# Contrast kernel on one core: the first 8 KB of each row as four row-interleaved loads, and tiles 6 to 11 loaded in pairs

## The chip, the core and the metric

The kernel runs on one core of a Trainium2 chip. The metric is device time in microseconds (us); before the change it is 239.09 us, the median of three runs (239.09 to 239.23). A profile shows one execution of the program, with its own span.

## What is computed

The input is 16 x 3 images of 512 x 512 float32. Each image is stretched about its own mean by a factor of 1.5 and clipped to 0..1:

```python
mean = np.mean(x, axis=(2, 3), keepdims=True)
return np.clip(mean + factor * (x - mean), 0, 1).astype(np.float32)
```

So an image's mean must be complete before its first pixel can be written. Input and output are 50.33 MB each, and every byte is moved once in each direction.

## The kernel before

**Tiles.** The 48 images are cut into 12 tiles of four images. A tile is 128 partitions (32 for each image) of one 8192-element row each, so 32 KB a partition and 4 MB (4096 KB) in all. The on-chip memory holds `ring`, six such tiles; tile t lies in slot t % 6, is loaded there, is changed in place and is stored from there.

**Work on one tile** (`compute`, lines 78 to 98). VectorE (DVE) adds up the first 4352 elements of each row (L81) while ScalarE (ACT) adds up the other 3840 (L84). Two small matmuls (L86, L87) against a constant block matrix add the sums of the 32 partitions of each image and give each partition its shift, (1 - factor) x mean. DVE then does multiply-and-add (L91) and clip (L94) over the whole row, and ACT issues the store (L101). For tile 0 alone the last three steps are done in two parts, of 2048 and 6144 elements. DVE and ACT take the tiles in order; ACT's instruction stream for a tile is sum, store, and then the sum of the next tile.

**Loads** (`load`, lines 68 to 76). All loads are issued by SyncE (SP) on one DMA queue (q1 in the profile), in the order written out by hand in lines 104 to 112; all stores are issued by ACT on a second queue (q10). Each load is one DMA with one completion: whoever reads any part of it waits until all of it has landed. With `n=2` one DMA fills two neighbouring slots, so both tiles count as landed together. At the start come five loads: the first 2048 elements of tile 0's rows, the other 6144, tile 1, tiles 2 and 3 as one, tiles 4 and 5 as one. Tile t + 6 goes to the slot of tile t, so its load must wait until the store of tile t has landed; it is written after `compute(t)`, for t = 0 to 5, which makes six single loads. SP executes in order: a load that waits holds up all later loads.

In what follows S8 is the store of tile 8, L8 the load of tile 8, and L4/5 a load of tiles 4 and 5 in one DMA. (The profile's own labels such as L81 are lines of the kernel; all of these are 63 or higher.)

Of the kernel before, what the change touches and what calls it, by code (L numbers as in the profile page):

```python
# [1 line left out]

# [4 lines left out]


P = 128  # L10
ROW = 8192
BUFS = 6
SHORT = 2048
FIRST = (SHORT, ROW - SHORT)
SUM = 4352


@with_exitstack
def kernel(
    ctx: ExitStack,  # L20
    tc: tile.TileContext,
    x: bass.AP,
    factor: float,
    out: bass.AP,
):

    nc = tc.nc
    f32 = mybir.dt.float32  # L30
    Alu = mybir.AluOpType
    Act = mybir.ActivationFunctionType

    B, C, H, W = x.shape
    n_img, n_pix = B * C, H * W
    ppi = n_pix // ROW
    per_tile = P // ppi
    n_tiles = n_img // per_tile
    assert ppi * ROW == n_pix and per_tile * n_tiles == n_img

    factor = float(factor)
    wconst = (1.0 - factor) / float(n_pix)

    x_f = x.rearrange("b c h w -> (b c h w)")
    out_f = out.rearrange("b c h w -> (b c h w)")

    def dram(ap, t, c0=0, c1=ROW):
        return bass.AP(tensor=ap.tensor, offset=t * P * ROW + c0, ap=[[ROW, P], [1, c1 - c0]])

    consts = ctx.enter_context(tc.tile_pool(name="consts", bufs=1))  # L50
    xpool = ctx.enter_context(tc.tile_pool(name="xpool", bufs=1))
    small = ctx.enter_context(tc.tile_pool(name="small", bufs=1))
    psum = ctx.enter_context(tc.tile_pool(name="psum", bufs=1, space=bass.MemoryType.PSUM))


    sums = small.tile([P, 2 * n_tiles], f32, name="sums")
    junk = small.tile([P, ROW - SUM], f32, name="junk")
    bias = psum.tile([P, n_tiles], f32, name="bias")

    blockw = consts.tile([P, P], f32, name="blockw")  # L60
    nc.gpsimd.memset(blockw, 0.0)  # L61
    for a in range(0, P, ppi):
        nc.gpsimd.memset(blockw[a : a + ppi, a : a + ppi], wconst)  # L63


    ring = xpool.tile([P, BUFS, ROW], f32, name="ring")

    def load(t, c0=0, c1=ROW, n=1):

        b = t % BUFS  # L70
        src = bass.AP(
            tensor=x_f.tensor,
            offset=t * P * ROW + c0,
            ap=[[ROW, P], [P * ROW, n], [1, c1 - c0]],
        )
        nc.sync.dma_start(out=ring[:, b : b + n, c0:c1], in_=src)  # L76

    def compute(t):
        xt = ring[:, t % BUFS, :]
        own = sums[:, 2 * t : 2 * t + 2]  # L80
        nc.vector.tensor_reduce(  # L81
            out=own[:, 0:1], in_=xt[:, 0:SUM], axis=mybir.AxisListType.X, op=Alu.add
        )
        nc.scalar.activation(out=junk, in_=xt[:, SUM:ROW], func=Act.Copy, accum_out=own[:, 1:2])  # L84
        shift = bias[:, t : t + 1]
        nc.tensor.matmul(shift, blockw, own[:, 1:2], start=True, stop=False)  # L86
        nc.tensor.matmul(shift, blockw, own[:, 0:1], start=False, stop=True)  # L87
        c = 0
        for n in FIRST if t == 0 else [ROW]:
            part = xt[:, c : c + n]  # L90
            nc.vector.tensor_scalar(  # L91
                out=part, in0=part, scalar1=factor, scalar2=shift, op0=Alu.mult, op1=Alu.add
            )
            nc.vector.tensor_scalar(  # L94
                out=part, in0=part, scalar1=0.0, scalar2=1.0, op0=Alu.max, op1=Alu.min
            )
            store(t, c, c + n)
            c += n

    def store(t, c0, c1):  # L100
        nc.scalar.dma_start(out=dram(out_f, t, c0, c1), in_=ring[:, t % BUFS, c0:c1])  # L101

    with tc.manual_schedule():
        load(0, c1=SHORT)
        load(0, c0=SHORT)
        load(1)
        load(2, n=2)
        load(4, n=2)
        for t in range(n_tiles):
            compute(t)  # L110
            if t + BUFS < n_tiles:
                load(t + BUFS)


# [1 line left out]
_INS = ['x', 'factor']  # L116
_OUTS = [((16, 3, 512, 512), 'float32')]

_NUMBERS = {'factor': 1.5}


# [26 lines left out]
```

## Time and profile before

| | us |
|---|---|
| median of 3 runs | 239.09 |
| span of the profiled execution | 237.3 |
| DVE busy in it | 163.1 (69%) |
| ACT busy | 43.2 (18%) |
| PE (matmul) busy | 14.1 (6%) |
| DMA queue q1 (loads), share of the 16 DMA engines' time | 49.7% |
| DMA queue q10 (stores) | 49.2% |
| DMA bytes, mean rate | 100.66 MB, 424 GB/s |

The profiled execution's span begins with the program's first instruction on the engines and ends with the last. The median, of other executions, lies 1.8 us above that span (239.09 - 237.27). A busy time is the sum over instructions; for DMA, the profile gives the share of the time of the 16 DMA engines, and for each issue the time from the issue to the landing of its last byte ("to landing"). The chain is followed backwards from the last instruction of the compute engines to whatever released it.

The landings, each from the DMA-issues view narrowed to one issue (issue time plus time to landing):

| DMA | issued | landed | | DMA | issued | landed |
|---|---|---|---|---|---|---|
| tile 0, first 8 KB | 0.74 | 5.5 | | S0, second part | 27.6 | 55.8 |
| L2/3 | 2.1 | 50.6 | | S1 | 41.9 | 76.4 |
| L4/5 | 2.8 | 87.6 | | S2 | 65.1 | 95.9 |
| L6 | 56.0 | 107.0 | | S3 | 79.4 | 115.2 |
| L7 | 76.6 | 126.2 | | S4 | 102.0 | 134.6 |
| L8 | 96.0 | 145.7 | | S5 | 116.3 | 154.0 |
| L9 | 115.3 | 165.0 | | S6 | 130.6 | 173.4 |
| L10 | 134.7 | 184.4 | | S7 | 144.9 | 192.8 |
| L11 | 154.2 | 203.7 | | S8 | 160.1 | 207.4 |
| | | | | S9 | 179.4 | 217.1 |
| | | | | S10 | 198.8 | 226.8 |
| | | | | S11 | 218.2 | 236.5 |

### The profile page before, as it was taken

What the parts mean: (1) busy time and instruction counts of PE and PEld (TensorE: products, weight loads), DVE (VectorE), ACT (ScalarE), POOL (GpSimd) and SP (SyncE); (2) the same over time, 40 slices, a digit from 0 to 9 for tenths busy, and PEclk for the clock granted to TensorE, in tenths of its full rate; (3) what the DMA queues carried; (4) which work ended last, traced back from release to release, by engine and by line L of the source; (5) the groups of instructions that cost most, each with busy time, mean ns of one, the idle gap of its engine ahead of it and who ended that gap; (6) DMA issues with size and microseconds to landing.
All of it is one profiled execution on the core that took longest, in us unless ns stands there. A gap on an engine that the chain in (4) does not pass through costs nothing.

```text
span 237.3 us, 285 instructions
## 1 busy us (share of the span) xinstructions
PE 14.1 (6%) x48; PEld 12.0 (5%) x48; DVE 163.1 (69%) x38; ACT 43.2 (18%) x25; POOL 0.9 (0%) x9
## 2 busy tenths in 40 slices
PE   0010010001010001010010100100100100010000
PEld 0010010001010001010010100100100100010000
DVE  0079989048989328999989898891892795687000
ACT  2050230041050023050320504101400500500000
POOL 1000000000000000000000000000000000000000
DMA  7999999999999999999999999999999999999996
GB/s 297 410 442 442 421 442 359 456 439 441 442 436 414 403 431 442 442 442 442 436 442 436 414 409 425 442 442 442 442 436 442 436 420 403 425 442 442 442 442 265
DMA packets 3712, 100.66 MB, mean 424 GB/s; under 512 B 384, under 2 KB 384, under 8 KB 384
## 3 DMA queue, kind: packets, MB, share of 16 engines
q1 hardware_dynamic: 1840, 50.33, 49.7%
q10 hardware_dynamic: 1872, 50.33, 49.2%
HBM read 50.33 MB, written 50.33 MB: 424 GB/s over the span
## 4 chain that ended last, share of the span: by engine, by line
DMA 57%; DVE 29%; another core or an unknown queue 3%; PE 1%; SPq 1%; issue 0%; DVEq 0%
DMA ring<-in_x_dram 41%; DMA out_dram<-ring 16%; DVE sums L81 10%; DVE ring L91 9%; DVE ring L94 9%; PE bias L87 1%; SPq L76 1%; DVEq L91 0%
## 5 line engine op out<-in xcount | busy, mean ns | idle before, releaser
L81 DVE TENSOR_REDUCE sums<-ring 128x1 f32<-128x4352 f32 x12 | 56.2, 4683 | 45.7 <-DMA ring<-in_x_dram 45.7
L84 ACT ACTIVATE junk<-ring 128x3840 f32<-128x3840 f32 x12 | 40.8, 3403 | 163.3 <-DMA ring<-in_x_dram 107.5
L91 DVE TENSOR_SCALAR ring<-ring,bias 128x8192 f32<-128x8192 f32 (+2 forms) x13 | 54.1, 4163 | 8.9 <-PE bias L87 7.4
L94 DVE TENSOR_SCALAR ring<-ring 128x8192 f32<-128x8192 f32 (+2 forms) x13 | 53.3, 4099 | 0.4
L86 PE MATMUL bias<-sums,blockw 128*128 128x1 f32 x24 | 7.0, 361 | 190.8 <-ACT junk L84 190.8
L86 PEld LDWEIGHTS bias<-sums,blockw 128*128 128x128 f32 x24 | 6.0, 312 | 191.7 <-ACT junk L84 175.2
L87 PE MATMUL bias<-sums,blockw 128*128 128x1 f32 x24 | 7.0, 363 | 4.3 <-DVE sums L81 3.9
L87 PEld LDWEIGHTS bias<-sums,blockw 128*128 128x128 f32 x24 | 6.0, 311 | 5.3 <-DVE sums L81 5.0
L84 ACT ACTIVATION_READ_ACCUMULATOR junk<-ring 128x1 f32 x12 | 2.2, 186 | 0.0
L84 ACT ACT_TABLE_LOAD x1 | 1.3, 1283 | 0.7 <-PEq L129 0.7
L63 POOL MEMSET blockw<- 32x32 f32 x4 | 0.5, 117 | 0.2
L61 POOL MEMSET blockw<- 128x128 f32 x1 | 0.2, 204 | 0.3 <-POOLq L129 0.3
L129 POOL MEMSET const-bfloat16-1.0<- 128x1 bf16 x1 | 0.1, 111 | 0.0
L129 POOL MEMSET const-uint8-127<- 128x1 uint8 x1 | 0.1, 111 | 0.0
L129 POOL MEMSET const-float32-1.0<- 128x1 f32 x1 | 0.1, 108 | 0.0
L129 POOL MEMSET const-float32-0.0<- 128x1 f32 x1 | 0.1, 103 | 0.2 <-issue 0.2
## 6 DMA issues: line engine op xcount, KB each, us to landing
out_dram<-ring ACTq DMA_DIRECT2D x11, 4096.0 KB, 35.8
ring<-in_x_dram SPq DMA_DIRECT2D x7, 4096.0 KB, 49.7
ring<-in_x_dram SPq DMA_DIRECT2D x2, 8192.0 KB, 66.7
ring<-in_x_dram SPq DMA_DIRECT2D x1, 3072.0 KB, 11.7
out_dram<-ring ACTq DMA_DIRECT2D x1, 3072.0 KB, 28.2
ring<-in_x_dram SPq DMA_DIRECT2D x1, 1024.0 KB, 4.8
out_dram<-ring ACTq DMA_DIRECT2D x1, 1024.0 KB, 17.5
```

The lines of the kernel that those rows point to most:

```text
L61: nc.gpsimd.memset(blockw, 0.0)
L63: nc.gpsimd.memset(blockw[a : a + ppi, a : a + ppi], wconst)
L76: nc.sync.dma_start(out=ring[:, b : b + n, c0:c1], in_=src)
L81: nc.vector.tensor_reduce(out=own[:, 0:1], in_=xt[:, 0:SUM], axis=mybir.AxisListType.X, op=Alu.add)
L84: nc.scalar.activation(out=junk, in_=xt[:, SUM:ROW], func=Act.Copy, accum_out=own[:, 1:2])
L86: nc.tensor.matmul(shift, blockw, own[:, 1:2], start=True, stop=False)
L87: nc.tensor.matmul(shift, blockw, own[:, 0:1], start=False, stop=True)
L91: nc.vector.tensor_scalar(out=part, in0=part, scalar1=factor, scalar2=shift, op0=Alu.mult, op1=Alu.add)
L94: nc.vector.tensor_scalar(out=part, in0=part, scalar1=0.0, scalar2=1.0, op0=Alu.max, op1=Alu.min)
L129: nc = _bacc.Bacc("TRN2", target_bir_lowering=False, num_devices=1)
```

## The change

Two things change, both in the loads. The first load of tile 0 (2048 elements of each of 128 rows, 1 MB) becomes four loads of 32 rows each, rows f, f+4, f+8 and so on for f = 0 to 3, 256 KB each. And the six single loads of tiles 6 to 11 become three loads of two tiles each, written after `compute(1)`, `compute(3)` and `compute(5)`. The work of the other engines is unchanged.

```diff
+STEP = 4
...
-    def load(t, c0=0, c1=ROW, n=1):
+    def load(t, c0=0, c1=ROW, n=1, first=0, step=1):
...
-            offset=t * P * ROW + c0,
-            ap=[[ROW, P], [P * ROW, n], [1, c1 - c0]],
+            offset=(t * P + first) * ROW + c0,
+            ap=[[step * ROW, P // step], [P * ROW, n], [1, c1 - c0]],
...
-        nc.sync.dma_start(out=ring[:, b : b + n, c0:c1], in_=src)
+        nc.sync.dma_start(out=ring[first:P:step, b : b + n, c0:c1], in_=src)
...
-        load(0, c1=SHORT)
+        for first in range(STEP):
+            load(0, c1=SHORT, first=first, step=STEP)
         load(0, c0=SHORT)
         load(1)
         load(2, n=2)
         load(4, n=2)
         for t in range(n_tiles):
             compute(t)
-            if t + BUFS < n_tiles:
-                load(t + BUFS)
+            if t % 2 and t + BUFS < n_tiles:
+                load(t + BUFS - 1, n=2)
```

In the compiled order of the changed kernel SP issues eleven loads, as many as before: four of 32x2048, one of 128x6144, one of 128x8192 and five of 128x2x8192. The load of tiles 4 and 5 also gains a wait for one of the four quarter loads, whose semaphore it uses again.

## The prediction

> **What bounds the kernel now.** I read the page first, for busy shares and the slices.
>
> ```profile
> span 237.3 us, 285 instructions
> ...
> DVE  0079989048989328999989898891892795687000
> ...
> DMA  7999999999999999999999999999999999999996
> GB/s 297 410 442 442 421 442 359 456 439 441 442 436 414 403 431 442 442 442 442 436 442 436 414 409 425 442 442 442 442 436 442 436 420 403 425 442 442 442 442 265
> ```
>
> The DMA engines have work in every slice, the last included, while DVE is idle in the last three. So the span is 100.66 MB pushed through full DMA engines, with a short start and a short end. Next, how fast they can go: the windows view (length, busy times, clock, DMA share, GB/s) and the DMA view of 107 to 202 us (packets, MB, share of the engines).
>
> ```profile
> 56.00:203.80 147.80, 9.39 (x33) 8.02 (x32) 117.43 (x27) 27.97 (x16) 0.00 (x0) 1.00 1.00 433
> 203.80:236.50 32.70, 1.18 (x4) 1.01 (x4) 13.56 (x3) 3.50 (x2) 0.00 (x0) 1.00 0.97 417
> ```
>
> ```profile
> q10 hardware_dynamic: 717, 20.87, 50.9%
> q1 hardware_dynamic: 703, 20.48, 49.9%
> ```
>
> While loads and stores are both queued, they share 433 GB/s half and half. The loads end at 203.7 (L11). From then on only stores are left, and they still fill 0.97 of the engines, because a backlog is waiting: S8 lands at 207.4, S9 at 217.1, S10 at 226.8, S11 at 236.5, 9.7 us apart, which is 4.19 MB at 433 GB/s. That backlog is what hides the work on the last tile. Last, the chain in order of time (start, length, what) and the timeline (start, length, engine, line; in brackets the idle time before).
>
> ```profile
> 154.17 49.57 DMA ring<-in_x_dram
> 203.73 0.02 issue
> 203.76 4.70 DVE sums L81
> ...
> 213.71 4.43 DVE ring L94
> ```
>
> ```profile
> 50.67 4.69 DVE L81 TENSOR_REDUCE sums<-ring 128x1 f32<-128x4352 f32 x1 [8.77 <-DMA ring<-in_x_dram]
> ...
> 102.00 0.34 ACTq L101 DMA_DIRECT2D out_dram<-ring  x1
> ...
> 116.30 0.34 ACTq L101 DMA_DIRECT2D out_dram<-ring  x1
> ```
>
> Tile 11 lands at 203.7 and its store is issued at 218.2: 14.4 us of work. S10, issued at 198.8, keeps the engines busy until 226.8, so S11 is in the queue 8.6 us before it is due. The start at 50.67 shows what a pair does: DVE had waited 8.77 us for L2/3, and tile 2 could not start before tile 3 had landed too. Two tiles that land together are worked on one after the other: L4/5 lands at 87.6, S4 goes out at 102.0, S5 at 116.3, so the second store is issued 28.7 us after the landing.
>
> **Part 1: pairs, the middle.** L6/7 must wait for S0 and S1, so it is issued when L7 was, at 76.6, not at 56.0. The load queue does not run dry: L4/5 occupies it until 87.6, 11 us longer. Likewise L8/9 goes out with S3's landing at 115.3, 10.9 us before L6/7 lands (126.2), and L10/11 at 154.2, 10.8 us before 165.0. Nothing is queued behind them on SP but the next such load. The loads thus keep their half share and L10/11 lands when L11 did, at 203.7. Tiles 6, 8 and 10 become available 19.4 us later than now (126.2, 165.0, 203.7 against 107.0, 145.7, 184.4).
>
> The stores follow: S6 at 126.2 + 14.4 = 140.6, S7 at 154.9, S8 at 179.4, S9 at 193.7. The store queue has work until S5 lands (154.0), S7 (192.8), S9 (217.1), so each pair's first store is 13 us early; this slack is the cover, and it costs nothing here. Three SP issues go away (0.34 us each), hidden behind a queue that is never empty: nothing.
>
> **Part 1: pairs, the end.** Here the cover is gone. Tiles 10 and 11 land together at 203.7. S10 is issued 14.4 us later, at 218.2, 1.1 us after S9 has landed: the engines stand idle. S11 is issued at 203.7 + 28.7 = 232.5, where DVE is now the bound. S10, alone, is through by about 218.2 + 2 + 9.7 = 230, so S11 also starts on idle engines and must pay in full the time from issue to landing.
>
> The trace has no store on idle engines. Its nearest row is the first load: issued at 0.74, 1 MB landed after 4.8 us, of which 2.4 us is 1.05 MB at 433 GB/s, which leaves 2.4 us. Counted by the bytes instead (254 GB/s from 2 to 3 us, 449 from 3 to 5.5, 1.38 MB by 5.5), the stream runs as if at full rate from 2.4, 1.7 us after the issue. So 1.7 to 2.4; I take **2.0**, since a store of 4 MB has room to even out its start. The tail after the last landing is 237.3 - 236.5 = 0.8.
>
> The sum: 203.7 + 28.7 + 2.0 + 9.7 + 0.8 = **244.9** as span, 7.6 over the profiled 237.3. The median lies 1.8 above that span, so 239.1 + 7.6 = **246.7**.
>
> **Part 2: the quarter loads.** The same bytes in four DMAs. SP's first issues start 0.46 us apart (0.74, 1.17, 1.64, 2.11), so three more put back the second load of tile 0 from 1.2 to 2.6. Its bytes are due when the first MB is through, at 5.5, 2.9 us after its issue, against 1.7 to 2.4 of latency: hidden, with 0.5 us to spare. If that cover is gone it costs at most 3 x 0.46 = 1.4. The other way, the first MB lands 0.7 us later than a stream at full rate would have it (2.4 against 1.7 above); a finer split can win back no more. I take nothing, between -0.7 and +1.4, since both ends are far from any row of a 32-row DMA and the stream is fed throughout. No compute waits for less than the whole of tile 0 (L81 and L84 read both parts), so no work starts earlier. L4/5's new wait ends with a quarter load, near 5 us, and its bytes are due at 50.6: nothing. The three additional semaphores that L81 waits for on tile 0 fall into the wait for the second part.
>
> [...] Back-to-back DMAs in the trace show no gap: the last four stores land 9.7 us apart, at full rate. [...]
>
> **Rivals.**
>
> *The loads win a larger share* (not slower). If pairs got more than half of the engines, L10/11 would land earlier and the stores' backlog would be longer. To hide both last tiles, S11 must be issued 2.0 us before S10 ends in an unbroken queue, at 226.8 - 2.0 = 224.8, so L10/11 must land at 196.1, 7.6 us earlier. From then on the bytes decide again: 239.1, or 238.4 with the start's 0.7. For it: L4/5 took 50.6 to 87.6 = 37.0 us, against 38.7 for two single loads. Against it: until 55.8 it ran beside tile 0's smaller store parts, and L10/11 would need 50.3 MB - 25.2 MB in 108.5 us in place of 116.1, 232 GB/s, 54% of the engines, where the view shows 49.9. Chance 4%.
>
> *Tile 10 does not wait for tile 11*, so the change does not do what it says: then S10 leaves at about 198.8, and it stays 239.1. Against it: the 8.77 us before tile 2. Chance 2%.
>
> *The quarter loads are lopsided*: 32 rows spread over only half of the engines. These would carry twice their share of the first MB, 2.4 us more, and every later landing waits for the slowest engine: 246.7 + 2.4 = 249.1. For it: no row shows a 32-row load. Against it: 32 divides by 16 as 128 does. Chance 8%. Something dearer at the start, beyond 249: 3%.
>
> **How the numbers follow.** The forecast, 246.7, has 83%. Its own bounds: store latency -0.3/+0.4, start -0.7/+1.4, and the loads' share at an even 50% in place of 49.9 of 100.8 (half a percent of 116 us, so 0.6 earlier): 245.1 to 248.5. The range is 245.1 to 249.1, which takes in the lopsided start. This kernel's measurement tells about 0.2% (0.5 us) from no change. Faster by more than that: 3%, most of the larger-share case, with the start's gain; same: 3%, the rest of that case and the one where tile 10 does not wait; slower: 94%.
>
> **What would show it.** Right: L6/7, L8/9, L10/11 issued near 76.6, 115.3 and 154.2; DVE idle about 10 us before tile 6; L10/11 landing near 203.7; store issues near 218.2 and 232.5; the DMA slices broken near 218 and 231, and the chain ending with two tiles of DVE work. Wrong: an L10/11 that lands more than 1 us off 203.7 (the share), a tile 0 that lands well after 12.9 (the start), S11 landing much over 12 us after its issue (the latency), or no gap between the last stores.

## The result and the profile after

The changed kernel takes 246.16 us (median of six runs, 244.66 to 246.92), against 239.22 us before (239.09 to 239.38): 1.0282 times the time, 95% interval 1.0255 to 1.0309. It is slower, by 6.9 us. Its profiled execution has a span of 242.7 us and is the fastest of the six; the other spans lie between 243.2 and 245.0. The page of the changed kernel, its span and slices:

```profile
span 242.7 us, 282 instructions
...
DVE  0048989238989428989408998607998806898900
...
DMA  6999999999999999999999999999999999999496
GB/s 213 385 428 432 398 432 439 448 420 444 432 432 432 432 432 432 437 432 432 432 432 432 432 432 432 432 432 432 437 432 437 432 432 437 437 421 432 178 421 270
```

The middle is as full as before (433 GB/s from 56 to 203 us in both). New are the weak first slices (213 and 385 GB/s, were 297 and 410) and the hole near the end (178 GB/s, digit 4), with VectorE (DVE) busy above it. The windows of the changed kernel (length, busy times, clock, DMA share, GB/s) show both; 449 GB/s was the rate of the first row's window before.

```profile
3.00:5.50 2.50, 0.00 (x0) 0.00 (x0) 0.00 (x0) 0.00 (x0) 0.00 (x0) 1.00 0.86 292
...
219.00:229.00 10.00, 1.17 (x4) 1.00 (x4) 9.23 (x3) 1.41 (x2) 0.00 (x0) 1.00 0.77 331
229.00:231.50 2.50, 0.00 (x0) 0.00 (x0) 1.78 (x1) 0.00 (x0) 0.00 (x0) 1.00 0.00 0
```

From 229.0 to 231.5 no packet starts: S10 landed at 228.7 and the DMA engines wait for tile 11. (A packet is counted in the window in which it starts, so the share of a short window can be over 1.00.) The timeline of the changed kernel tells why (the end of each line is the idle time before and what ended it):

```profile
127.09 4.69 DVE L82 TENSOR_REDUCE sums<-ring 128x1 f32<-128x4352 f32 x1 [8.87 <-DMA ring<-in_x_dram]
...
164.60 4.69 DVE L82 TENSOR_REDUCE sums<-ring 128x1 f32<-128x4352 f32 x1 [8.85 <-DMA ring<-in_x_dram]
...
202.11 4.69 DVE L82 TENSOR_REDUCE sums<-ring 128x1 f32<-128x4352 f32 x1 [8.85 <-DMA ring<-in_x_dram]
...
216.52 0.34 ACTq L102 DMA_DIRECT2D out_dram<-ring  x1
...
230.81 0.34 ACTq L102 DMA_DIRECT2D out_dram<-ring  x1
```

The three pairs land at 127.1, 164.6 and 202.1, DVE idle 8.9 us before each. S10 goes out 14.4 us after the last landing, S11 28.7 us after it. S10 leaves 2.6 us before S9 has landed (219.1), so the engines run through to it without a hole; the one hole is the one before S11. The DMA-issues view narrowed to S11:

```profile
out_dram<-ring ACTq DMA_DIRECT2D x1, 4096.0 KB, 11.1
```

230.8 + 11.1 = 241.9, and the span ends 0.8 later. The chain of this profile reaches back only to 221.1, to the last two DVE steps of tile 11; what stands before them has to be read from the timeline.

### The profile page after: what moved, and what is told of

Its sections match the earlier page's. It is cut to its first block, busy times and chain, and to the rows that moved or that the text cites. A ratio compares the mean times of both kernels' runs of the same rounds, so it can differ in the third digit from the quotient of the medians.

```text
span 242.7 us, 282 instructions
## 1 busy us (share of the span) xinstructions
PE 14.0 (6%) x48; PEld 12.0 (5%) x48; DVE 163.0 (67%) x38; ACT 43.2 (18%) x25; POOL 0.9 (0%) x9
```

## The experiments

Each time stands beside the kernel before, measured on the same chip in the same series (239.2 to 239.3 us). Differences below are between medians.

### The two parts alone: pairs_only and quarters_only

`pairs_only` is the changed kernel with the first load undone, `quarters_only` the one with the pairs undone:

```diff
 pairs_only
-        for first in range(STEP):
-            load(0, c1=SHORT, first=first, step=STEP)
+        load(0, c1=SHORT)
 quarters_only
-            if t % 2 and t + BUFS < n_tiles:
-                load(t + BUFS - 1, n=2)
+            if t + BUFS < n_tiles:
+                load(t + BUFS)
```

> Pairs for tiles 6 to 11, the first load whole as before. Theory A (the quarter loads lost about 2 us at the start, and the pairs cost the rest at the end): L10/11 lands near 200.0, that is 2.1 before the 202.1 of the changed kernel, S11 is issued 28.7 later, near 228.7, the span is near 240.6 and the time near 242.5 to 244. Theory B (the quarters cost nothing, the pairs everything): the span of the changed kernel again, 242.7, and its time, 246.2.

> Quarter loads of the first MB, single loads for tiles 6 to 11. Theory A: the stores' backlog still covers the last tile, the bytes decide, and the 2.0 to 2.3 us by which tile 0 came later (15.2 against 12.9) are paid in full: 241.2 to 241.5. Theory B: 239.2.

Measured: pairs_only 242.97 us (241.3 to 243.1), ratio 1.0142 (1.0117 to 1.0167); quarters_only 243.0 us (242.21 to 243.64), ratio 1.0154 (1.0135 to 1.0174). Each part alone costs 3.8 us, and theory B is out: the quarters cost as much as the pairs. In pairs_only the pair lands where theory A had it; its timeline:

```profile
125.24 4.69 DVE L82 TENSOR_REDUCE sums<-ring 128x1 f32<-128x4352 f32 x1 [8.82 <-DMA ring<-in_x_dram]
...
162.76 4.68 DVE L82 TENSOR_REDUCE sums<-ring 128x1 f32<-128x4352 f32 x1 [8.86 <-DMA ring<-in_x_dram]
...
200.34 4.69 DVE L82 TENSOR_REDUCE sums<-ring 128x1 f32<-128x4352 f32 x1 [8.92 <-DMA ring<-in_x_dram]
...
229.04 0.34 ACTq L102 DMA_DIRECT2D out_dram<-ring  x1
```

Two readings: the pairs come 37.5 us apart, where two single loads took 38.7 (2 x 19.4), so that L10/11 lands at 200.3 and not at 203.7; and S11 again goes out 28.7 us after that.

quarters_only lost more than the 2.0 to 2.3 that I had read off the landing of tile 0. Its last microseconds show where the rest is, first of quarters_only and then of before:

```profile
226.00:234.00 8.00, 0.00 (x0) 0.00 (x0) 0.00 (x0) 0.00 (x0) 0.00 (x0) 1.00 1.02 442
234.00:236.00 2.00, 0.00 (x0) 0.00 (x0) 0.00 (x0) 0.00 (x0) 0.00 (x0) 1.00 0.91 393
236.00:238.00 2.00, 0.00 (x0) 0.00 (x0) 0.00 (x0) 0.00 (x0) 0.00 (x0) 1.00 0.46 197
```

```profile
234.00:235.00 1.00, 0.00 (x0) 0.00 (x0) 0.00 (x0) 0.00 (x0) 0.00 (x0) 1.00 1.21 524
235.00:236.50 1.50, 0.00 (x0) 0.00 (x0) 0.00 (x0) 0.00 (x0) 0.00 (x0) 1.00 0.01 0
```

Before, all 16 DMA engines stop within 0.6 us of each other (the table below). With the quarters some have finished while others have several packets left, and the rate falls away over some 3 us. The last store is done when the slowest engine is done: that engine finishes S11 3.0 us later than before, the fastest one 0.4, and the span is 3.6 longer.

### How the first load is split: block_quarters, halves_only, column_quarters

`block_quarters` takes 32 neighbouring rows at a time, `halves_only` has two loads of every second row (`STEP = 2`), `column_quarters` has four loads of all 128 rows. All have single loads for tiles 6 to 11.

```diff
 block_quarters
-        for first in range(STEP):
-            load(0, c1=SHORT, first=first, step=STEP)
+        for first in range(0, P, P // STEP):
+            load(0, c1=SHORT, first=first, step=STEP)
...
-            ap=[[step * ROW, P // step], [P * ROW, n], [1, c1 - c0]],
+            ap=[[ROW, P // step], [P * ROW, n], [1, c1 - c0]],
...
-        nc.sync.dma_start(out=ring[first:P:step, b : b + n, c0:c1], in_=src)
+        nc.sync.dma_start(out=ring[first : first + P // step, b : b + n, c0:c1], in_=src)
 column_quarters
-        load(0, c1=SHORT)
+        for c in range(0, SHORT, SHORT // 4):
+            load(0, c0=c, c1=c + SHORT // 4)
```

> As the run with quarter loads alone, but each quarter is 32 neighbouring rows, not every fourth. If the number of DMAs is what costs (each is issued 0.6 us after the last and starts on idle engines), 241.2 to 241.5 as with the interleaved quarters. If the step of four between rows is what makes an issue take 0.57 in place of 0.42, the issues come 0.46 apart and the time is 239.6 to 240.2.

> The first MB as two loads of every second row, the rest as before. If the quarters cost because each is issued 0.63 us after the last and holds only 0.6 us of data, halves (1.2 us of data each) keep the engines fed: 239.2 to 239.6. If they cost because their rows are spread otherwise over the DMA engines than those of a whole load, halves cost about the same, 241.5 to 243.

> The first MB as four loads of all 128 rows, 512 elements each, the rest as before. As many DMAs of the same size as the row quarters. If the number of DMAs costs, 241 to 243. If the row split costs (a slower issue, 0.57 for 0.42, and rows spread otherwise over the DMA engines), 239.2 to 239.8.

Measured, with the times at which the first and the last of the 16 DMA engines finish (from the trace's records of the engines' completions, counted from the first packet):

| kernel | time, us | ratio (95%) | tile 0's load: first, last engine | S11: first, last engine |
|---|---|---|---|---|
| before | 239.2 | | 10.2, 10.7 | 233.7, 234.3 |
| halves_only | 240.71 | 1.0064 (1.0046 to 1.0081) | 10.6, 11.8 | 233.8, 235.4 |
| column_quarters | 241.48 | 1.0087 (1.0067 to 1.0108) | 10.7, 12.5 | 233.9, 236.3 |
| quarters_only | 243.0 | 1.0154 (1.0135 to 1.0174) | 11.2, 13.5 | 234.1, 237.4 |
| block_quarters | 240.8 | 1.0061 (1.0049 to 1.0074) | 12.2, 12.6 | 235.0, 235.5 |

Only column quarters keep to one of my two causes (241 to 243, the number of DMAs); blocks and halves lie outside both ranges that I had given. Column quarters cost 2.2 us although SP issues them 0.47 apart in 0.42 each as before, so cutting this load into more DMAs costs. Quarters of every fourth row cost 1.6 us more, and they are issued 0.62 apart, each issue taking 0.54 to 0.59, so the row split costs too; halves cost 1.4, more than the "fed" theory allowed and less than the "spread" theory. The long issues go with the step between the rows: SP issued the quarters of neighbouring rows 0.46 apart, in 0.42 each.

What the table does show is the form of the loss. In the three other splits (halves, columns, quarters of every fourth row) the fastest engine finishes S11 where it did before, within 0.4 us; the slowest one is late by 1.1, 2.0 and 3.0 us, after 1.0, 1.7 and 2.8 in tile 0's load. With the first packet, which starts 2.1 us after the span's start where rows are stepped over and 1.7 before, that is nearly the whole of the longer span (quarters_only 3.6). Most of what the slowest engine loses in the first 12 us is therefore still missing at the end: from 56 to 203 us the engines of quarters_only are full (share 1.00), as before the change, which leaves little room to catch up. The records do not name the engine; that it is the same one is inferred from the 16 finishing times of a DMA, which keep much the same distances from one DMA to the next (in quarters_only the latest four are 1.4 to 2.3 us behind the first in tile 0's load, 1.7 to 3.3 in S11).

The neighbouring rows are another case: all engines are late together, by 1.8 to 2.0 us in tile 0's load and by 1.2 in S11, so some was caught up here. The windows of before and of block_quarters say that they were busy but slow, at half the rate:

```profile
3.00:5.50 2.50, 0.00 (x0) 0.00 (x0) 0.00 (x0) 0.00 (x0) 0.00 (x0) 1.00 1.07 449
...
3.00:5.50 2.50, 0.00 (x0) 0.00 (x0) 0.00 (x0) 0.00 (x0) 0.00 (x0) 1.00 1.00 220
```

In the trace's records an 8 KB packet of this first MB takes 606 ns (median), against 309 in all the row-interleaved kernels and before. So the packets of 32 neighbouring rows take twice as long. Why is not shown: the blocks read neighbouring rows of the input and write neighbouring partitions, and no run parts the two. A step between the rows keeps the packets at 309 ns, but it loses more than that in another place: 243.0 us against 240.8 for the blocks, with longer issues and uneven engines. How these two are connected no run shows.

### The end: last_two_single, last_pair_only, no_clip_11

`last_two_single` has pairs for tiles 6 to 9 and single loads for 10 and 11, `last_pair_only` the reverse; both have the first load of before. `no_clip_11` is the changed kernel with the last tile's clip left out.

```diff
 last_two_single
-            if t % 2 and t + BUFS < n_tiles:
+            if t in (1, 3):
                 load(t + BUFS - 1, n=2)
+            elif t in (4, 5):
+                load(t + BUFS)
 last_pair_only
-            if t % 2 and t + BUFS < n_tiles:
+            if t < 4:
+                load(t + BUFS)
+            elif t == 5:
                 load(t + BUFS - 1, n=2)
 no_clip_11
-            nc.vector.tensor_scalar(
-                out=part, in0=part, scalar1=0.0, scalar2=1.0, op0=Alu.max, op1=Alu.min
-            )
+            if t < n_tiles - 1:
+                nc.vector.tensor_scalar(
+                    out=part, in0=part, scalar1=0.0, scalar2=1.0, op0=Alu.max, op1=Alu.min
+                )
```

> First load whole, pairs for tiles 6/7 and 8/9, single loads for tiles 10 and 11. Theory A (what costs is only that tiles 10 and 11 land together, with no stores left behind which to hide the second of them): 239.2, with L11 landing near 201.3, 2.4 earlier than before, since each pair took 1.2 us less than two singles. If a pair also costs in the middle, more than 240.

> First load whole, single loads for tiles 6 to 9, one pair for tiles 10 and 11. If every pair wins the loads 1.2 us (16 packets against 15) and only the last pair costs at the end, this one pays the end with only one gain: L10/11 lands near 202.5, 2.4 later than with three pairs (200.3), S11 is issued near 231.2, and the time is 2 above that of the three pairs (242.97), near 245. Rival: if each pair costs something of its own and the last is a third of it, less than 242.97, near 240.5.

> The changed kernel with the clip of tile 11 (4.43 us on VectorE) left out, so the last tile is not clipped. If the end is set by VectorE working off two tiles that landed together, S11 is issued 4.4 earlier and the time falls by 4.4, to about 241.8. Rival: if the end is set by S10 and S11 on the DMA engines, S11 still starts when S10 is through, 2 us before its present start, and the time falls by 2 at most.

Measured: last_two_single 239.96 us, ratio 1.0029 (1.0020 to 1.0038), with a span of 237.3, that of before, and L11 landing at 201.2; last_pair_only 245.12 us, ratio 1.0245 (1.0232 to 1.0258); no_clip_11 242.02 us (240.81 to 242.43), 4.1 below the changed kernel. The timelines of last_pair_only and of no_clip_11:

```profile
202.66 4.69 DVE L82 TENSOR_REDUCE sums<-ring 128x1 f32<-128x4352 f32 x1 [23.14 <-DMA ring<-in_x_dram]
...
231.35 0.34 ACTq L102 DMA_DIRECT2D out_dram<-ring  x1
```

```profile
203.12 4.69 DVE L82 TENSOR_REDUCE sums<-ring 128x1 f32<-128x4352 f32 x1 [8.84 <-DMA ring<-in_x_dram]
...
227.34 0.34 ACTq L103 DMA_DIRECT2D out_dram<-ring  x1
```

So, within the span, the whole cost of the pairs is that tiles 10 and 11 land together. One pair there costs 5.8 us (245.12 against 239.32); pairs elsewhere cost nothing within the span, and in front of a last pair they even help, since each lands the later loads 1.2 us earlier: three pairs cost 3.8. That the end of the changed kernel hangs on DVE's work on tile 11 is seen in its empty window: DVE clips tile 11 from 226.35 to 230.78, and the engines stand still from 229.0. no_clip_11 agrees: S11 goes out 24.2 us after the landing in place of 28.7, 2.4 us before S10 has landed (229.7), and lands at 239.4, 9.7 after it, with no hole left. The 4.1 us alone would not decide it. The runs of the changed kernel lie 2.3 us apart; by the two profiles, from the landing of L10/11 to that of S11, 3.5 us are saved (36.3 in place of 39.8), and that is where the DMA engines take over again. The "2 at most" of the rival counted S11's wait for its issue and not the start-up of 1.4 us (11.1 against 9.7) that an unbroken queue hides as well.

### Turns on the DMA engines: two_dma_loads

`two_dma_loads` is the kernel before (with the `load` of the changed one) with each of tiles 6 to 11 loaded by two DMAs of 64 rows.

```diff
             if t + BUFS < n_tiles:
-                load(t + BUFS)
+                for first in range(2):
+                    load(t + BUFS, first=first, step=2)
```

> As before the change, but each of tiles 6 to 11 is loaded by two DMAs of 64 rows (every second row). Theory of turns: loads and stores take turns on each DMA engine, and the completion of a DMA takes a turn as a packet does; a pair has 1 completion for 16 packets, a store 1 for 8, which gives the loads 16 turns of data against 15 for stores in 37.5 us. Here loads have 2 completions for 8 packets, so they must fall behind: 17 packets, 20.6 us a tile in place of 19.4, and L11 lands 6.5 to 7.3 later than 203.7, near 210.5; the bytes still decide and the time is 239.2 to 240. Rival (the pair's gain comes from something else): L11 lands near 203.7.

Measured: 244.07 us, the middle of three runs from 242.43 to 244.34 (a fourth took 246.39), ratio 1.0180 (1.0148 to 1.0212). The loads do fall behind, as only the theory of turns had it, and by more than it said. The timeline of two_dma_loads:

```profile
193.44 4.69 DVE L82 TENSOR_REDUCE sums<-ring 128x1 f32<-128x4352 f32 x1 [7.57 <-DMA ring<-in_x_dram]
...
214.81 4.69 DVE L82 TENSOR_REDUCE sums<-ring 128x1 f32<-128x4352 f32 x1 [6.98 <-DMA ring<-in_x_dram]
```

L11 lands at 214.8, not at 210.5, and the distance is 21.4 us a tile. The records of the single engines split this in two. The earliest engine completes tiles 6 to 9 20.6 us apart, the 17 packets of the theory (a 32 KB packet takes 1.21 us), and L11 at 206.0 after the first packet, 6.2 later than before (199.9). The latest one is at 212.6: the engines have come apart by 6.6 us, which I had not expected and cannot explain from these runs. That made the time miss my 239.2 to 240: S11 left at 229.2, when some engines had run dry, but S10 landed only at 231.7, and S11 at 241.3, 9.6 after it. The slowest engine still had a backlog, so the end is again that of the slowest engine. In the middle the engines are as full as before (433 GB/s in most slices of the page), so the loads lost share and not time.

The trace of the kernel before shows the turn of the completion directly. The DMA views of three windows of one packet's time each, from 161.2, 162.42 and 163.64 to 164.85 us, have most engines in step (packets, MB, share):

```profile
q10 hardware_dynamic: 15, 0.49, 93.2%
q1 hardware_dynamic: 1, 0.03, 6.2%
...
q10 hardware_dynamic: 16, 0.52, 99.5%
q1 hardware_dynamic: 15, 0.00, 0.7%
...
q1 hardware_dynamic: 16, 0.49, 94.0%
q10 hardware_dynamic: 1, 0.03, 6.3%
```

In the first it is the stores' turn. In the second it is that of the loads, but 15 engines send only the completion of L9, which takes 0.7% of the engines' time, and the stores go a second time; in the third the loads go on. So here a turn is one record of the trace, of 32 KB or of a completion's 4 bytes; the page of before counts 384 packets under 512 B, 16 for each of its 24 DMAs. From one landing to another the two queues have equal numbers of packets: 288 each from 126.2 to 165.0 us before the change (L7 to L9), and 272 each from 127.1 to 164.6 us of the changed kernel (L6/7 to L8/9), 256 of data and 16 completions for the loads (8.39 MB), 240 and 32 for the stores (7.86 MB). That is the 16 to 15 of the pairs (37.5 us = 31 packets of 1.21), and the 17 packets of two_dma_loads agree with it.

### Fewer DMAs at the start: tile_0_whole and one_first_load

`one_first_load` loads tile 0 with one DMA, `tile_0_whole` also stores it with one.

```diff
-        load(0, c1=SHORT)
-        load(0, c0=SHORT)
+        load(0)
 tile_0_whole also
-FIRST = (SHORT, ROW - SHORT)
+FIRST = (ROW,)
```

> As before the change, but tile 0 is loaded by one DMA and stored by one, 24 DMAs in all in place of 26. If every DMA that the start is cut into lets some DMA engines fall behind (2 DMAs for tile 0's load: 239.2, 3 with halves: 240.7, 5 with quarters: 243.0 and 241.5), fewer should save a little: 238.3 to 239.0. If the start before is already as even as it gets, 239.2. Tile 0's store comes 6 us later, which costs nothing as long as the engines have loads to move.

> Only tile 0's load is one DMA, its store stays in two parts. As for the run with tile 0 whole in both; the difference of the two tells what the store's two parts cost: 0 to 0.5 us.

Measured: tile_0_whole 240.12 us (239.49 to 241.76), ratio 1.0046 (1.0026 to 1.0065); one_first_load 240.05 us, ratio 1.0030 (1.0018 to 1.0042). (The kernel before has 24 DMAs, 11 loads and 13 stores, and tile_0_whole 22; the 26 and 24 of my expectation were miscounted.) Nothing is won: the profiled spans are 237.6 both, against 237.3, and other runs of tile_0_whole have spans of up to 239.7. The two medians differ by 0.07 us, so the store's two parts cost nothing that shows. The loss does not simply grow with the number of DMAs; two for tile 0 is the best of the numbers tried. No kernel here beats the one before.

## Why the prediction was right, and where not

**Slower, and the pairs' end as a reason: right, but it is half of the loss.** The prediction's steps for the pairs can be checked one by one. DVE's wait before each pair: 8.9 us, where it said about 10. The issues of the pairs' loads: at 78.6, 118.5 and 158.4, later than the 76.6, 115.3 and 154.2 that it gave, because S1, S3 and S5 landed later; but each still 6 us or more before the load ahead had landed, so the load queue did not run dry. Nothing lost in the middle: shown by last_two_single, within the span. "S11 is issued at 203.7 + 28.7": the 28.7 is there to the tenth in three kernels. The idle engines before S11: the empty window from 229.0 to 231.5. The idle engines before S10: not there. S10 was to leave 1.1 us after S9 had landed; it left at 216.5, and S9 landed at 219.1, 2.0 us later than before. The sum goes through DVE and not through S10, so this cost the forecast nothing.

**The landing of L10/11 was mis-sized.** I had it at 203.7, on a half share that does not change. The DMA view of the changed kernel from 107 to 200 us (packets, MB, share):

```profile
q1 hardware_dynamic: 671, 20.55, 51.1%
q10 hardware_dynamic: 684, 19.79, 49.3%
```

Before, it was 49.9 for loads and 50.9 for stores. That is the rival of the larger share, come true for less than half of the 7.6 us that it needed: pairs alone bring the landing to 200.3, 3.4 us earlier. The row that spoke for it, L4/5 in 37.0 us, was the right one: the measured pairs come 37.5 apart. The 49.9% that was set against it had been taken from single loads.

**The start-up of S11 was mis-sized.** 11.1 - 9.7 = 1.4 us in place of 2.0, below both of my ends (1.7 to 2.4). The lower end left out the bytes that had moved before 2 us. The row of that window stands in the profile of before with 33 GB/s: with these 0.07 MB it is 1.44 MB by 5.5, which at 433 GB/s puts the start at 2.2, 1.4 us after the issue.

**The quarters at nothing: wrong.** The step that failed is "hidden, with 0.5 us to spare", with its bound of +1.4. I took the spacing of the issues (0.46) from whole-row loads; quarters by rows come 0.62 apart with 0.6 us of data in each (256 KB at 433 GB/s). And I counted the loss as a delay of the stream, where most of it is one of single engines, which the mean rate shows only in part: alone the quarters cost 3.8 us (ratio 1.0154, 1.0135 to 1.0174). The lopsided rival had the right form, a later end because of the slowest engine, with 2.4 us and another cause. The 9.7 us from each of the last four stores to the next, which the prediction sets beside the quarters, tell of a full queue and not of the start: there four DMAs in place of one cost 2.2 us even as column quarters.

**The sum.** On the profiled execution: 202.1 + 28.7 + 1.4 + 9.7 + 0.8 = 242.7, where I had 244.9. L10/11 is 1.6 early: 3.4 gained by the pairs' share, 1.8 lost by the quarters (202.1 against 200.3). That 246.7 lies so close to the median of 246.16 is luck. The pairs, to which the forecast gave the whole 7.6 us, alone take 242.97 us, 3.7 below it; the quarters, to which it gave nothing, add 3.2 to that (246.16 against 242.97). The two errors have opposite signs. Two of the prediction's own signs of being wrong came true as well: L10/11 more than 1 us off 203.7, and tile 0 landing at 15.2, well after 12.9.

**Open.** Why runs of the changed kernel and of pairs_only differ by 2 us, when last_pair_only keeps within 0.3. What makes single engines slow at the start: the records show 8 KB packets of up to 1.17 us (usually 0.31) until 4 us after the first packet and 24 KB packets of up to 1.91 us (usually 0.91) until 9 us in quarters_only, and slow 8 KB packets until 2 us before the change, but not the cause. And 0.6 us of last_two_single that lies outside its span (239.84 for a span of 237.3; before 239.15 for 237.3).

## What to carry to other kernels

In a kernel bound by DMA, ask which transfers are still queued when a load lands, since they hide the work on it: here two tiles in one DMA landed together, and the second's work was covered only while a backlog of stores lasted (one pair at the end cost 5.8 us), so keep the last loads single. Look at the slowest DMA engine and not at the mean rate, since here the slowest engine's loss at the start was for the most part still there at the end (quarters_only: 2.8 us in tile 0's load, 3.0 in S11). Before cutting a load into more DMAs, take the issue time and the data per issue from loads of the same shape.

## What the runs showed of the hardware

- A DMA's completion takes a turn of its own against the other queue, though hardly any time: while 15 engines sent the completions of L9 (0.7% of the engines' time in 1.22 us), the stores moved 16 packets right after 15. Loads with one completion for 16 packets moved 16 packets for 15 of the stores, loads with two for 8 packets had 17 packets' time to a tile on the earliest engine.
- Loads of 32 neighbouring rows took 606 ns for an 8 KB packet, loads of every fourth row 309.
- At the start SP needed 0.54 to 0.59 us to issue a load of every second or fourth row, 0.58 for a load of all rows right behind those, and else 0.37 to 0.43 for one of all rows of one tile or of 32 neighbouring ones.
- A 4 MB store on idle engines landed 11.1 us after its issue, 1.4 more than its 9.7 us in a full queue.
